# One expert's x in fp32 by SyncE instead of two by SyncE and ScalarE, and the other one in the GpSimd queue

## The chip, the core and the metric

The kernel runs on one core of a Trainium2 chip. The metric is the device time of one execution in microseconds (us); lower is better. A core has five engines that run side by side: TensorE (PE in the profile, with its weight loads as PEld), VectorE (DVE), ScalarE (ACT), GpSimd (POOL) and SyncE (SP). Data come and go by 16 DMA engines that all queues share. In this kernel three engines issue transfers: SyncE and ScalarE each into a queue whose descriptors hardware makes (q1 and q10 in the profile), GpSimd into a queue whose descriptors its own cores write (q0). Only the transfers that GpSimd issues convert fp32 to fp16 on the way.

## The reference

Eight experts, each with 256 rows of x, a hidden size of 512 and an inner size of 2048. All inputs and the output are fp32.

```python
n_experts, capacity, hidden, expert_hidden = 8, 256, 512, 2048
# x (8, 256, 512), w1 (8, 512, 2048), w2 (8, 2048, 512), b1 (8, 2048), b2 (8, 512)
h = np.matmul(x, w1) + b1[:, np.newaxis, :]
h = np.maximum(h, 0)
return (np.matmul(h, w2) + b2[:, np.newaxis, :]).astype(np.float32)
```

## The kernel before

**Data.** Each expert has 4 MB of w1 and 4 MB of w2 in fp32 and 512 KB of x. The kernel multiplies in fp16. `load_w1` (L73) and `load_w2` (L79) fetch a whole expert's weights in one transfer from GpSimd, which writes 2 MB of fp16; `load_x` (L67) does the same with x and writes 256 KB. Three buffers hold w1, three hold w2, four hold x in fp16 (`x16`).

**Two experts' x come another way.** For experts 0 and 1 (`nXF32 = 2`) x is fetched as it stands, in fp32, into the tile `x32` (L188): expert 0's by SyncE, expert 1's by ScalarE. VectorE then copies each into its `x16` tile (L201, a cast). ScalarE also issues the fetch of b1 (L189), as 16 rows of 1024 numbers.

**Work on an expert.** `transposes(e)` (L96) turns x on TensorE by eight products with a unit matrix, and VectorE copies the result to `xT` (L106). `first_product(e)` (L108) makes 16 blocks of h with four products each (L113); ScalarE adds b1 and clips at zero (L120). Midway, after block 8, it calls `transposes(e + 1)`. `second_product(e)` (L151) puts b2 into two sums (L163) and adds 32 products of h and w2 (L175); VectorE and ScalarE copy the sums out (L138, L139). The second product runs three experts behind the first (`LAG = 3`).

**Before the first product** b1 must be turned as well: 64 small products with a unit matrix (L206), which GpSimd makes (`make_identity`, shown as masks.py:197 and 199), and two copies (L214). These stand ahead of `transposes(0)` on TensorE.

**The order of the transfers** is written out by hand. GpSimd issues w1 of expert 0 and b2 (L191) first, then makes the two unit matrices, and then takes the list `ring` in order: w1 of expert 1, x of expert 2, w1 of expert 2, x of expert 3, w1 of expert 3, w2 of expert 0, and so on. Outputs of seven experts are written back from the same list (`flush`, L130), and w2 of expert 7 comes in eight pieces (L88). GpSimd holds an issue back until the buffer is free and until the transfer eight places earlier in its queue has landed, as the kernel's eight completion semaphores for this queue are used in turn. The output of expert 7 leaves from SyncE and ScalarE (L142, L143, L149).

Of the kernel before, what the change touches and what calls it, by code (L numbers as in the profile page):

```python
# [11 lines left out]
def kernel(  # L12
# [9 lines left out]
    nc = tc.nc  # L22
# [5 lines left out]
    nTB = T // P  # L28
# [4 lines left out]
    LATE = (5, 6)  # L33
    RING = (0, 1, 2, 3, 4) + LATE
    PARTS = {}
    nXF32 = 2

    def ordered(ins):
        return tc.keep_in_program_order(ins)
# [17 lines left out]
    b1_rows = singles.tile([E * 2, M // 2], fp32)  # L57
# [15 lines left out]
    def load_w1(e):  # L73
        w1_sb[e] = w1_pool.tile([P, nKC, M], fp16, tag="w1", name="w1sb")
        ordered(nc.gpsimd.dma_start(  # L75
            out=w1_sb[e], in_=w1[e].rearrange("(p kc) m -> p kc m", kc=nKC)
        ))
# [107 lines left out]

    x32 = singles.tile([P, nXF32, nTB, H], fp32)
    for e in range(nXF32):
        (nc.sync if e == 0 else nc.scalar).dma_start(out=x32[:, e], max_dma_last_dim=2048, in_=x[e].rearrange("(p tb) h -> p tb h", tb=nTB))  # L188
    nc.scalar.dma_start(out=b1_rows, in_=b1.rearrange("e (s i) -> (e s) i", s=2))  # L189
    load_w1(0)  # L190
    ordered(nc.gpsimd.dma_start(  # L191
        out=b2_sb,
        in_=b2.rearrange("e h -> (e h)").rearrange("(o f) -> o f", o=1),
# [10 lines left out]
    for j in range(nJ):  # L204
        for s in range(2):
            ordered(nc.tensor.matmul(  # L206
                out=pb[s * 64 : (s + 1) * 64, j, :, :],
# [5 lines left out]
    for s in range(2):  # L213
        nc.vector.tensor_copy(  # L214
            out=b1T[s * 64 : (s + 1) * 64, :, :], in_=pb[s * 64 : (s + 1) * 64, :, :, s]
# [15 lines left out]
    e = E - LAG - 1  # L231
# [50 lines left out]
```

## Time and profile before

| | |
|---|---|
| time, median of 4 runs | 183.41 us (183.28 to 183.55) |
| the profiled execution: its time, and its span from first to last instruction | 183.55 us, 181.8 us |
| PE, PEld busy | 139.5 us (77%), 99.2 us (55%) |
| ACT, POOL, DVE busy | 62.9 us, 22.1 us, 13.4 us |
| moved by DMA, counted where it is written | 40.58 MB in 7017 packets |
| read from and written to HBM | 71.39 MB, 4.19 MB |
| granted TensorE clock | 0.924 of full speed |

The times of instructions and transfers are from this one profiled execution, counted from the start of its span; 1.75 us of its time lie outside the span. A packet is what one DMA engine moves in one go. The share of a queue is the time that its packets took, divided by 16 engines and by the stretch of time; packets overlap a little at their ends, and a packet counts in the stretch where it starts, so that a short stretch can show more than 100%.

### The profile page before, as it was taken

How to read it: one execution, taken by the hardware profiler on the slowest of the kernel's cores; microseconds unless marked ns; L12 is line 12 of the kernel's file. 1: busy time of each engine (PE TensorE's matmuls, PEld its weight loads, DVE VectorE, ACT ScalarE, POOL GpSimd, SP SyncE). 2: the span in 40 equal slices, each digit the busy share in tenths (PEclk: the TensorE clock that was granted, in tenths of full speed). 3: DMA queues.
4: the chain of work that ended last, by engine and by line, in shares of the span. 5: the costliest groups of instructions: out<-in, count | busy, mean ns of one | idle time of the engine just before them, and what ended most of it. 6: DMA issues, size and time to landing. Idle time of an engine off the chain costs nothing.

```text
span 181.8 us, 2204 instructions
## 1 busy us (share of the span) xinstructions
PE 139.5 (77%) x946; PEld 99.2 (55%) x946; DVE 13.4 (7%) x22; ACT 62.9 (35%) x138; POOL 22.1 (12%) x46
## 2 busy tenths in 40 slices
PE   0555999489650999649991899909999994999990
PEld 0544889479540845637481754907559641334670
DVE  0320011001000101010100101001010010000110
ACT  0022689548560421706063240723309501010100
POOL 7100021300300011111010000200004003113300
PEclk9999999979995699979999579996999999699999
DMA  5999999999999989999999999999999999999995
GB/s 182 280 195 225 231 209 195 209 253 213 193 231 231 213 191 231 198 234 202 231 231 191 213 231 231 173 288 206 198 231 224 274 195 278 211 242 282 218 279 191
DMA packets 7017, 40.58 MB, mean 223 GB/s; under 512 B 1216, under 2 KB 2256, under 8 KB 4960
## 3 DMA queue, kind: packets, MB, share of 16 engines
q0 software_dynamic: 5872, 38.81, 97.8%
q1 hardware_dynamic: 688, 0.95, 1.7%
q10 hardware_dynamic: 448, 0.69, 1.0%
q8 instruction: 7, 0.11, 0.2%
q14 instruction: 2, 0.02, 0.0%
HBM read 71.39 MB, written 4.19 MB: 416 GB/s over the span
## 4 chain that ended last, share of the span: by engine, by line
DMA 58%; PE 24%; issue 9%; another core or an unknown queue 3%; POOL 2%; ACT 0%; POOLq 0%
DMA x<-in_x_dram 24%; DMA w2sb<-in_w_dram 21%; PE acc L175 17%; DMA w1sb<-in_w_dram 13%; PE ph L113 6%; PE acc L163 1%; PE psx L100 1%; POOL w2sb L85 1%; POOL w1sb L75 1%; POOL out_dram L132 0%; POOL b_sb L191 0%; POOL ident masks.py:199 0%; POOL ident masks.py:197 0%; ACT out L139 0%
## 5 line engine op out<-in xcount | busy, mean ns | idle before, releaser
L113 PE MATMUL ph<-xT,w1sb 128*128 128x256 f16 x512 | 69.3, 302 | 8.7 <-DMA w1sb<-in_w_dram 8.7
L120 ACT ACTIVATE hT<-ph,b1T 128x256 f16<-128x256 f32 x128 | 57.1, 474 | 43.6 <-PE ph L113 43.4
L113 PEld LDWEIGHTS <-w1sb 128*128 128x128 f16 x512 | 62.1, 149 | 15.1 <-DMA w1sb<-in_w_dram 9.6
L175 PE MATMUL acc<-w2sb,hT 128*128 128x512 f16 x224 | 51.2, 388 | 2.3 <-DMA w2sb<-in_w_dram 2.3
L175 PEld LDWEIGHTS <-hT 128*128 128x128 f16 x288 | 27.6, 99 | 32.8 <-issue 7.7
L139 ACT COPY out<-acc 128x512 f32<-128x512 f32 (+2 forms) x9 | 4.9, 541 | 60.1 <-PE acc L175 60.1
L100 PE MATMUL psx<-ident,x 128*128 128x128 f16 x64 | 6.6, 265 | 20.1 <-DMA x<-in_x_dram 19.5
L100 PEld LDWEIGHTS <-x 128*128 128x128 f16 x64 | 5.3, 128 | 21.2 <-DMA x<-in_x_dram 20.4
L75 POOL DMA_DIRECT2D w1sb<-in_w_dram x8 | 4.4, 554 | 60.3 <-PE ph L113 59.5
L106 DVE COPY xT<-psx 128x1024 f16<-128x1024 f16 x8 | 5.5, 692 | 81.8 <-PE psx L100 81.8
L138 DVE COPY out<-acc 128x512 f32<-128x512 f32 (+2 forms) x9 | 5.7, 632 | 73.5 <-PE acc L175 73.5
L85 POOL DMA_DIRECT2D w2sb<-in_w_dram x8 | 4.3, 536 | 48.8 <-PE acc L175 48.8
L206 PE MATMUL pb<-ident,b_rows 16*64 16x16 f32 x64 | 3.7, 265 | 6.7 <-DMA b_rows<-in_b_dram 6.7
L175 PE MATMUL acc<-w,hT 128*128 128x320 f16 (+1 forms) x64 | 7.3, 273 | 0.0
L206 PEld LDWEIGHTS pb<-ident,b_rows 16*64 16x64 f32 x64 | 3.6, 198 | 6.7 <-issue 6.7
L91 POOL DMA_DIRECT2D w<-in_w_dram x8 | 5.0, 621 | 12.5 <-DMA w2sb<-in_w_dram 9.6
L132 POOL DMA_DIRECT2D out_dram<-out x7 | 3.8, 541 | 22.0 <-ACT out L139 13.1
L120 ACT ACT_TABLE_LOAD x1 | 1.3, 1283 | 11.1 <-DVE b1T L214 11.1
L163 PE MATMUL acc<-b_sb,ones 1*128 1x512 f16 (+2 forms) x18 | 4.8, 355 | 0.0
L69 POOL DMA_DIRECT2D x<-in_x_dram x6 | 3.3, 545 | 6.1 <-DMA w2sb<-in_w_dram 5.6
L163 PEld LDWEIGHTS <-ones 1*128 1x128 f16 x18 | 1.1, 92 | 2.2 <-issue 2.1
L201 DVE CAST x<-x 128x1024 f16<-128x1024 f32 x2 | 1.4, 694 | 4.4 <-DMA x<-in_x_dram 4.3
(9 smaller groups left out, 2.6 us busy)
## 6 DMA issues: line engine op xcount, KB each, us to landing
w1sb<-in_w_dram POOLq DMA_DIRECT2D x8, 2048.0 KB, 33.7
w2sb<-in_w_dram POOLq DMA_DIRECT2D x6, 2048.0 KB, 46.1
out_dram<-out POOLq DMA_DIRECT2D x7, 512.0 KB, 28.3
w2sb<-in_w_dram POOLq DMA_DIRECT2D x2, 1024.0 KB, 25.3
x<-in_x_dram POOLq DMA_DIRECT2D x6, 256.0 KB, 39.0
w<-in_w_dram POOLq DMA_DIRECT2D x2, 384.0 KB, 19.2
x<-in_x_dram SPq DMA_DIRECT2D x1, 512.0 KB, 4.5
x<-in_x_dram ACTq DMA_DIRECT2D x1, 512.0 KB, 5.3
```

What stands on the lines that cost most here:

```text
L75: ordered(nc.gpsimd.dma_start(out=w1_sb[e], in_=w1[e].rearrange("(p kc) m -> p kc m", kc=nKC)))
L85: ordered(nc.gpsimd.dma_start(out=t[:, lo : lo + step, :], in_=src[:, lo : lo + step, :]))
L91: ordered(nc.gpsimd.dma_start(out=t, in_=src[:, lo:hi, c0:c1]))
L100: ordered(nc.tensor.transpose(out=pt[:, kc, tb * P : (tb + 1) * P], in_=x16[e][:, tb, :].rearrange("p (q kc) -> p q kc", kc=nKC)[:, :, kc] ...
L106: nc.vector.tensor_copy(out=xT[e], in_=pt)
L113: ordered(nc.tensor.matmul(out=ph, lhsT=w1_sb[e][:, kc, :].rearrange("p (q j) -> p q j", j=nJ)[:, :, j], rhs=xT[e][:, kc, :], start=(kc == 0),
L120: nc.scalar.activation(out=hT[e][:, j, :], in_=ph, func=mybir.ActivationFunctionType.Relu, bias=b1T[:, j, e : e + 1], scale=1.0,)
L138: nc.vector.tensor_copy(out=out_sb[:, 0, :], in_=po[0])
L139: nc.scalar.copy(out=out_sb[:, 1, :], in_=po[1])
L163: ordered(nc.tensor.matmul(out=t, lhsT=ones1, rhs=b2_sb[0:1, e * H + c0 : e * H + c1], start=True, stop=False,))
L175: ordered(nc.tensor.matmul(out=acc[c0, tb], lhsT=hT[e][:, j, tb * P : (tb + 1) * P], rhs=t[:, j - lo, c0 - p0 : c1 - p0], start=False, sto ...
L206: ordered(nc.tensor.matmul(out=pb[s * 64 : (s + 1) * 64, j, :, :], lhsT=b1_rows.rearrange("r (q j) -> r q j", j=nJ)[:, :, j], rhs=ident[0 ...
```

## The change

`nXF32` becomes 1. Expert 0's x is fetched by SyncE in fp32 as before, and the fetch of b1 goes to SyncE behind it. ScalarE issues no transfer at the start any more. Expert 1's x is fetched by `load_x(1)`, which becomes the first entry of `ring`: GpSimd issues it ahead of w1 of expert 1, and it is converted on the way. The `x32` tile is half as large, and one cast on VectorE is gone. In the changed kernel's list of instructions by engine, SyncE has one more, ScalarE two fewer, VectorE one fewer and GpSimd one more; TensorE has the same in the same order.

```diff
-    nXF32 = 2
+    nXF32 = 1
...
     x32 = singles.tile([P, nXF32, nTB, H], fp32)
     for e in range(nXF32):
-        (nc.sync if e == 0 else nc.scalar).dma_start(out=x32[:, e], max_dma_last_dim=2048, in_=x[e].rearrange("(p tb) h -> p tb h", tb=nTB))
-    nc.scalar.dma_start(out=b1_rows, in_=b1.rearrange("e (s i) -> (e s) i", s=2))
+        nc.sync.dma_start(
+            out=x32[:, e], max_dma_last_dim=2048, in_=x[e].rearrange("(p tb) h -> p tb h", tb=nTB)
+        )
+    nc.sync.dma_start(out=b1_rows, in_=b1.rearrange("e (s i) -> (e s) i", s=2))
     load_w1(0)
```

## The prediction

> **What bounds the kernel now.** I read the page's rows by slice and queue first, then the chain that ended last, then the timeline and the DMA queues of the first microseconds, because only those are touched.
>
> From the page: the busy share of the 16 DMA engines in 40 slices of 4.5 us, and the queues with packets, MB and share of the span.
>
> ```profile
> DMA  5999999999999989999999999999999999999995
> q0 software_dynamic: 5872, 38.81, 97.8%
> q1 hardware_dynamic: 688, 0.95, 1.7%
> q10 hardware_dynamic: 448, 0.69, 1.0%
> ```
>
> After the first slice the DMA engines never rest, and GpSimd's queue q0 fills them. Twenty-microsecond stretches from 40 to 160 us give a DMA share of 0.99 to 1.04. So the end moves with the sum of what the engines carry and with the time at which they begin, not with any one wait of TensorE. The chain of waits, in order of time (start, duration, what), agrees:
>
> ```profile
> 3.29 22.90 DMA w1sb<-in_w_dram
> ...
> 114.94 38.31 DMA w2sb<-in_w_dram
> 153.25 0.04 issue
> 153.29 8.75 PE acc L175 x32
> ```
>
> The long links are transfers waiting in the queue behind others. From 153.29 TensorE works almost without a pause until 177.4, but the start of that stretch is set by a landing of w2, and the last piece of w2 lands at 176.8, just ahead of its products. If q0 as a whole shifts, both shift.
>
> The timeline of the start (start, duration, engine, operation, in brackets the idle time before):
>
> ```profile
> 0.74 0.43 SPq L188 DMA_DIRECT2D x<-in_x_dram  x1
> 0.74 0.50 ACTq L188 DMA_DIRECT2D x<-in_x_dram  x1
> 1.26 0.67 POOL L75 DMA_DIRECT2D w1sb<-in_w_dram  x1 [0.81 <-POOLq L266]
> 1.27 0.49 ACTq L189 DMA_DIRECT2D b_rows<-in_b_dram  x1
> 15.58 6.85 PE L113 MATMUL ph<-xT,w1sb 128*128 128x256 f16 x36 [3.44 <-DMA w1sb<-in_w_dram]
> ```
>
> GpSimd has issued expert 0's w1 by 1.93. But the queues show when its packets move. First the stretch 1.5 to 2.9 us, then 3.0 to 4.5 (packets, MB, share):
>
> ```profile
> q1 hardware_dynamic: 80, 0.16, 63.2%
> q10 hardware_dynamic: 6, 0.01, 4.1%
> ```
>
> ```profile
> q1 hardware_dynamic: 149, 0.31, 52.1%
> q10 hardware_dynamic: 145, 0.30, 51.4%
> ```
>
> And the stretch 5.14 to 5.45, the first one in which q0 appears at all:
>
> ```profile
> q0 software_dynamic: 16, 0.26, 406.5%
> q10 hardware_dynamic: 35, 0.04, 35.1%
> ```
>
> From 3.0 on x of both experts fills all 16 engines, 294 packets in 1.5 us. The first 16 packets of q0, one for each engine, start in the 0.3 us in which q10 (x of expert 1, then b1) runs out. Before 2.9 the engines were not full and q0 moved nothing, so w1 became ready somewhere between 2.9 and 5.14; the trace does not say where. This is the open number.
>
> **The change part by part.**
>
> *Expert 1's x leaves the hardware queue.* It is 512 KB in packets of 2 KB, 256 of them. At 294 packets in 1.5 us, 196 a microsecond, they take 256 / 196 = 1.31 us of all engines. Without them x of expert 0 and b1 run out 1.31 us earlier: instead of about 5.3 (the middle of the stretch above) at about 4.0.
>
> *The slow beginning.* In 1.5 to 2.9 only 86 packets start, with a share of 67%; the stretch 2.5 to 3.0 has 62%, so 0.19 us there are idle, in which expert 0's x alone does not fill the engines. Descriptors for both x's are being made in that time. If those of expert 1 no longer compete, part of it may come back: 0 to 0.19, and I take 0.1. So the engines would be free for q0 at about 3.9.
>
> *Expert 1's x enters q0 between b2 and expert 1's w1.* The price has a row: expert 2's x does the same in this trace, behind expert 1's w1. Of the issues in the stretch 2.9 to 3.9 (KB each, us from issue to landing):
>
> ```profile
> w1sb<-in_w_dram POOLq DMA_DIRECT2D x1, 2048.0 KB, 22.9
> x<-in_x_dram POOLq DMA_DIRECT2D x1, 256.0 KB, 23.6
> ```
>
> The first was issued at 3.29 and landed at 26.2; the second, issued at 3.85, landed at 27.45. The x in the ring cost 1.25 us. Its packets give nearly the same: in 24.9 to 25.7 all of q0's packets but three are of this x, 80 in 0.8 us, and 128 of them (half of 256, as fp16 is half as long) take 1.28. I take 1.25.
>
> *When w1 is ready.* If by 3.9, q0 starts as soon as the engines are free, and no time is lost. If later, the engines rest until then. Bounds: ready at 2.9, cost 0; ready only at 5.15, cost 5.15 - 3.9 = 1.25. I take 0, by the nearest rows: SyncE's x was issued from 0.74 and its first packets come in the stretch 1.5 to 2.0, about 1 us later. ScalarE's, issued at the same time, appears only at the end of 1.5 to 2.9, some 2 us later. For q0, ready at 3.9 would be 2.6 us from the issue at 1.26, more than either; ready at 5.15 would be 3.9.
>
> On this the Trainium skill can be heard, in "DMA: Bandwidth & Descriptors". Its table of specifications gives the first byte of a GpSimd transfer as about 1 us and of a SyncE one as about 0.6; the first is an estimate of readiness near 2.9 from the end of issue at 1.93, and by it the gap is nothing. Its section on queues, rings and completion order says that a DMA engine takes turns between the queues that have work, packet by packet. That speaks against this change: a w1 that was ready at 3 would have had turns between the packets of x, and the trace shows none before 5.14. By that rule w1 was not ready earlier, the gap is 1.25, and the sum would be slower by 1.1. I do not follow it, because with q0 ready by chance on each engine just as that engine's last x or b1 packet ended, some engine should show a pause, and from 5.14 to 6.3 the shares of q0 (108.6%) and q10 (9.4%) leave no room for one.
>
> *Issues moved.* On SyncE b1 is issued behind x (0.43 us), at about 1.2 instead of 1.27; nothing else is on SyncE until 177. ScalarE loses two issues that ended at 1.76; its first work is at 11.1. GpSimd's issue of 0.55 us for x moves w1 of expert 1 from 3.29 to 3.84, and those behind it likewise; expert 0's w1 keeps the engines busy long after that, and GpSimd's next issue waits for TensorE at 26.24 anyway. All at nothing. The semaphores used in turn move by one place, and each later issue waits for the same partner as before; only expert 4's w1 now follows x of expert 1 instead of b2, both landed long before 34.2.
>
> *VectorE and TensorE.* One cast of 0.69 us goes, off the path: TensorE waited for b1 (6.6), not for it. b1 ends about 1.3 earlier, and the chain b1 (3.7 us), copies, `transposes(0)`, copy to `xT` ends near 11.5 instead of 12.9; w1 lands near 14.2 instead of 15.5. The cover of 2.7 us stays. Expert 1's x lands about 15.5 (w1, then 1.25), and is wanted at block 8 of the first product, 6.6 us after 14.2. Cover 5 us; nothing. If the chain to `xT` lost its cover, TensorE would start late, but would still wait for expert 1's w1 at 26.2, as now (0.3 us).
>
> **Sum.** -1.31 - 0.10 + 1.25 + 0 = -0.16 us. Expert 1's w1 lands where it does now, 26.2, or 0.1 to 0.2 earlier, and so does all behind it. The profiled execution would go from 183.55 to 183.4; it lies 0.14 above the median, so the median goes from 183.41 to 183.25. No change that a measurement of this kernel can tell: that needs 0.2%, 0.37 us.
>
> **Rivals.**
>
> *Slower: a hole ahead of w1.* Same trade, but q0 is not ready at 3.9. It costs what it is late: 0.5 us late gives -0.16 + 0.5, 183.75; at worst -0.16 + 1.25 = +1.1, 184.5. It decides against the kernel from a readiness of about 4.45 on (0.37 + 0.16 behind 3.9). For it: q0 shows nothing before 5.14, although three queues could share. Against: the first packets of q0 come on the heels of q10.
>
> *Faster: the slow beginning shrinks.* In 1.8 to 2.9 the engines started 86 packets where full speed would be 216, so 0.66 us of them is lost to the start. If the hardware serves one x much better than two, all of that could come back: -1.31 - 0.66 + 1.25 = -0.7, 182.7. For it: x of expert 0 moves at half speed until x of expert 1 sets in. Against: the first packets are slow before x of expert 1 is in flight. Over 0.37 it needs the engines free, and w1 ready, by 3.7.
>
> *Slower for another reason.* TensorE's clock falls below full speed in some slices; another such stretch after 153 would push the end by itself, as the last stretch has no slack. Or x of expert 1 lands too late, which would need 5 us. Some tenths each, up to 184.2.
>
> **Chances.** The forecast's case has 0.53: most of it (0.43) within 0.37 us, 0.10 faster, as the term of 0.1 may be larger. The slow beginning 0.12, faster. The hole 0.30 and the other reasons 0.05, slower. That makes 0.22 faster, 0.43 no change, 0.35 slower. The forecast's own range is 182.95 to 183.6. The range for 8 in 10 goes to 182.9, which leaves out the far end of the faster rival, and to 184.4, which leaves out the last of the hole.
>
> **What would show it.** Right: q0's first packets near 3.9 with no idle stretch before, w1 of expert 0 landing near 14.2, x of expert 1 about 1.25 later, the products of expert 1 starting at 26.1 to 26.2, span 181.6. The hole: DMA idle between about 4 and the first packet of q0, and expert 1's products later than 26.24 by as much as the hole. Faster: q0's packets before 3.7. Wrong in another way: w1 of expert 1 lands on time and yet the end moves.

## The result, and the profile after

The change made the kernel slower: 184.56 us (median of 34 runs, 183.54 to 185.63) against 183.49 us (54 runs, 183.18 to 184.15), a ratio of 1.0052 with a 95% interval of 1.0042 to 1.0062, about 1 us. The forecast was 183.25 and no change. The changed kernel's runs lie in a band of 2.1 us, those of before in one of 1.0, and its best runs come within 0.1 us of before's median: what was lost is not a fixed amount. The profiled execution took 184.49 us with a span of 182.7 us, 0.9 us longer than before.

From the page of the changed kernel, the DMA engines' busy tenths and the queues (packets, MB, share of the span):

```profile
DMA  7989999999999999999999998999999999999994
q0 software_dynamic: 6016, 39.07, 98.3%
q1 hardware_dynamic: 720, 1.02, 1.7%
q10 hardware_dynamic: 144, 0.10, 0.2%
```

The move was made as described: q10 has lost 0.59 MB, q0 has gained 0.26 MB and 144 packets, and the first slice is busier, 7 tenths instead of 5, because q0 starts earlier. The engines are nearly always busy, as before. Nothing here tells of a loss.

The timeline of the changed kernel (start, duration, engine, operation, idle time before), the start and the first products of experts 0 and 1:

```profile
1.24 0.45 SPq L191 DMA_DIRECT2D b_rows<-in_b_dram  x1
1.25 0.67 POOL L75 DMA_DIRECT2D w1sb<-in_w_dram  x1 [0.81 <-POOLq L268]
3.29 0.56 POOL L69 DMA_DIRECT2D x<-in_x_dram  x1
15.87 6.46 PE L113 MATMUL ph<-xT,w1sb 128*128 128x256 f16 x36 [5.24 <-DMA w1sb<-in_w_dram]
...
26.87 4.16 PE L113 MATMUL ph<-xT,w1sb 128*128 128x256 f16 x36 [1.03 <-DMA w1sb<-in_w_dram]
```

w1 of expert 0 was to land near 14.2, earlier by the 1.3 us that left the hardware queues. TensorE begins at 15.87, later than the 15.58 of before, and the products of expert 1, forecast for 26.1 to 26.2, begin at 26.87. The timeline of before has there:

```profile
26.24 4.16 PE L113 MATMUL ph<-xT,w1sb 128*128 128x256 f16 x36 [0.30 <-DMA w1sb<-in_w_dram]
```

Now the queues in four consecutive stretches of the changed kernel; first 3.4 to 4.0 us:

```profile
q0 software_dynamic: 14, 0.23, 188.9%
q1 hardware_dynamic: 74, 0.12, 53.3%
```

4.0 to 4.4 us (q0's line alone here and in the next two):

```profile
q0 software_dynamic: 2, 0.03, 62.6%
```

4.5 to 5.4 us:

```profile
q0 software_dynamic: 15, 0.25, 132.2%
```

6.6 to 7.3 us:

```profile
q0 software_dynamic: 1, 0.02, 11.0%
```

This is where the time went. 16 first packets, one for each DMA engine: 14 start between 3.56 and 4.0, on the heels of x and b1, even a little earlier than forecast. The last one starts at 4.36 and takes 2726 ns, where all the other first packets take 1226 to 1391 ns. So 15 engines are at their second packet by 5.4 us, and the sixteenth comes to its second one at 7.06, the lone packet of the last stretch. In before, all 16 first packets started within 0.3 us and took 1226 to 1346 ns.

The records of the single packets say more. The hardware queue has 32 packets of 4 bytes here, 16 for x and 16 for b1, which I read as the close of each engine's part of a transfer. Of the 16 that close b1, 15 are followed by a first packet of q0 within 0.02 us. The one left over is the earliest and ends at 3.54. The trace does not number the engines, but by this the sixteenth was the first to run out of work, stood idle for 0.8 us until 4.36, and then needed 1.5 us more than the shortest for its first packet. In before no engine pauses: each of the 16 first packets starts as one of b1's closing packets ends, to within 0.01 us.

What one late engine means is seen in the landings. The trace counts the completion of a transfer engine by engine; the table gives when the first, the fifteenth and the last engine were through (us):

| | before | after |
|---|---|---|
| w1 of expert 0 | 15.13 / 15.53 / 15.54 | 13.73 / 14.17 / 15.82 |
| w1 of expert 1 | 24.88 / 25.24 / 26.20 | 24.73 / 26.21 / 26.82 |
| last piece of w2 | 175.20 / 176.78 / 176.82 | 175.17 / 177.03 / 177.74 |

The first engine is where the sum put it, 0.15 us ahead of before at w1 of expert 1 and level at the end. Before has one engine 0.96 us behind the fifteenth there, at 26.20; after's fifteenth, 26.21, may be the same one. The last engine is 0.6 to 0.9 us behind, and a transfer has landed when its last engine is through: TensorE starts at 15.87, behind 15.82. The Trainium skill says the same, "DMA: Bandwidth & Descriptors", section on why a DMA increments its semaphore by 16: the engines finish independently and each posts its own count. The table agrees, with 2.09 us between the first and the last engine.

The chain of waits of the changed kernel and its last stretch in the timeline:

```profile
3.84 22.98 DMA w1sb<-in_w_dram
...
154.55 19.21 DMA w<-in_w_dram
173.76 0.04 issue
173.80 2.89 PE acc L175 x24
```

```profile
171.95 1.47 PE L175 MATMUL acc<-w,hT 128*128 128x320 f16 x12 [0.75 <-DMA w<-in_w_dram]
173.80 4.47 PE L175 MATMUL acc<-w,hT 128*128 128x320 f16 x36 [0.38 <-DMA w<-in_w_dram]
```

In before TensorE ran from 153.29 almost without a pause, and had all 64 products of these pieces in one stretch:

```profile
170.06 7.29 PE L175 MATMUL acc<-w,hT 128*128 128x320 f16 x64
```

Now the pieces come too late for it twice, 0.75 and 0.38 us, and the last products end 0.92 us later, as the last landing does.

That the end follows the last landing holds for every kernel below. In all 19 profiled executions, time less landing of the last piece's last engine is 6.69 to 6.82 us (before 183.55 - 176.82 = 6.73, after 184.49 - 177.74 = 6.75), while the times go from 183.20 to 187.10.

### The profile page after: what moved, and what is told of

The parts are those of the page before. It is cut to its first block, busy times and chain, and to the rows that moved or that the text cites. A ratio compares the mean times of both kernels' runs of the same rounds, so it can differ in the third digit from the quotient of the medians.

```text
span 182.7 us, 2203 instructions
## 1 busy us (share of the span) xinstructions
PE 138.1 (76%) x946; PEld 98.5 (54%) x946; DVE 12.7 (7%) x21; ACT 62.7 (34%) x138; POOL 22.8 (12%) x47
## 3 DMA queue, kind: packets, MB, share of 16 engines
HBM read 71.39 MB, written 4.19 MB: 414 GB/s over the span
## 4 chain that ended last, share of the span: by engine, by line
DMA 71%; PE 22%; POOL 2%; issue 1%; ACT 1%; ACTq 0%; POOLq 0%
DMA x<-in_x_dram 24%; DMA w2sb<-in_w_dram 24%; DMA w1sb<-in_w_dram 13%; PE ph L113 11%; DMA w<-in_w_dram 11%; PE acc L175 10%; PE psx L100 1%; PE acc L163 1%; POOL w1sb L75 1%; ACT out L139 1%; POOL ident masks.py:199 0%; POOL out_dram L132 0%; POOL b_sb L193 0%; POOL w L91 0%; POOL x L69 0%
## 5 line engine op out<-in xcount | busy, mean ns | idle before, releaser
L175 PE MATMUL acc<-w2sb,hT 128*128 128x512 f16 x224 | 49.5, 379 | 1.1 <-DMA w2sb<-in_w_dram 1.1
L175 PEld LDWEIGHTS <-hT 128*128 128x128 f16 x288 | 27.1, 98 | 32.0 <-issue 6.1
L175 PE MATMUL acc<-w,hT 128*128 128x320 f16 (+1 forms) x64 | 7.8, 272 | 1.2 <-DMA w<-in_w_dram 1.1
L69 POOL DMA_DIRECT2D x<-in_x_dram x7 | 3.8, 547 | 5.9 <-DMA w2sb<-in_w_dram 4.5
L203 DVE CAST x<-x 128x1024 f16<-128x1024 f32 x1 | 0.7, 742 | 3.7 <-DMA x<-in_x_dram 3.7
```

The lines of the kernel that those rows point to most:

```text
L175: ordered(nc.tensor.matmul(out=acc[c0, tb], lhsT=hT[e][:, j, tb * P : (tb + 1) * P], rhs=t[:, j - lo, c0 - p0 : c1 - p0], start=False, sto ...
```

## The experiments

Theories for the late engine, with the letters that the expectations use:

- **A**: GpSimd issues x and w1 from 3.29 to 6.08, just when q0 now starts, and that disturbs it.
- **B**: q0 starts too soon after its own issue, and is not ready on every engine.
- **C**: b1 behind x on SyncE, on one hardware queue.
- **D**: no late engine matters; x in the ring costs more than 1.25 us.
- **E**: the hand-over from a hardware queue that runs out to q0.
- **F**: the time since the program began.
- **G**: what stands ahead of q0: one hardware queue that runs dry soon, instead of two.

Ratios are to before, measured beside it on the same chip, with 95% intervals.

**1. Later issues in the changed kernel (`after_hold`).** GpSimd waits for b1's copy before it goes on with the ring, so its issues come from 9.32 us on.

```diff
 transposes(0)
+hold = singles.tile([1, 1], fp32)
+ordered(nc.gpsimd.tensor_copy(out=hold, in_=b1T[0:1, 0, 0:1]))
```

> The changed kernel, but GpSimd copies one number of b1T (ready at 9.5 us in the changed kernel's trace) before it issues x of expert 1 and what follows, so that it issues nothing between 2.4 and 9.5 us, while q0 starts. Theory A (GpSimd's issues at 3.29 to 6.08 us, made while q0 starts at 3.55 to 4.36, hold up one of the 16 DMA engines, whose first q0 packet took 2726 ns against 1226 to 1391 on the others): no such packet, w1 of expert 0 lands near 14.3 us instead of 15.8, expert 1's products start near 26.1, and the time is some 0.2 us under before, 183.3, with runs within 0.3 us of each other. Theory B (q0's first packets are slow on one engine because they no longer stand ready behind another transfer, whoever issues then): the slow first packet stays, w1 lands at 15.5 to 16 and the time stays near 184.5 with the same spread.

Measured: 184.84 us (6 runs, 184.04 to 185.53), 1.0066 (1.0042 to 1.0090). First packets of up to 2036 ns with no issue near them. The profiled execution is the fastest of the six, and its last engine landed w1 of expert 0 at 14.71, which neither theory had named; by the times of all six A falls.

**2. Issues at q0's start in the kernel before (`before_late_issue`).** The reverse: they are put on 5.85 us and later, where before's first packets run.

```diff
+hold = singles.tile([1, 1], fp32)
+ordered(nc.gpsimd.tensor_copy(out=hold, in_=x32[0:1, 0, 0, 0:1]))
```

> The kernel before, but GpSimd copies one number of x32 of expert 0 (landed at 5.26 us in the trace of before) before it issues w1 of expert 1 and the three transfers behind it. They then fall into about 5.4 to 7.6 us, while q0 starts (5.15 to 5.42), instead of 3.29 to 5.44. Theory A: one engine's first or second q0 packet becomes slow here too, w1 of expert 0 lands up to 1.5 us after 15.5, and the time grows by 0.5 to 1.2 us with a wider spread, to about 184.3. Theory B: w1's packets still stand ready behind x of expert 1, and nothing changes: 183.5.

Measured: 183.55 us (11 runs), 0.9999 (0.9990 to 1.0007). A falls again.

**3. The old cover with the new ring (`after_cover`).** ScalarE fetches expert 1's x in fp32 as before, into a tile that nobody reads, and b1 behind it; x of expert 1 also stays in the ring.

```diff
+spare = singles.tile([P, nTB, H], fp32)
-nc.sync.dma_start(out=b1_rows, ...)
+nc.scalar.dma_start(out=spare, max_dma_last_dim=2048, in_=x[1].rearrange(...))
+nc.scalar.dma_start(out=b1_rows, ...)
```

> The changed kernel, but ScalarE also fetches x of expert 1 in fp32 as before, into a tile that nothing reads, and b1 behind it. q0 then starts near 5.3 us as in before, and only the 1.25 us of expert 1's x in q0 are added. Both theories: first packets of q0 all near 1226 ns; w1 of expert 0 at 15.5, expert 1's products 1.25 us later than in before, at 27.5; time before + 1.25 = 184.7, narrow spread. If the x in q0 cost much less or more than 1.25, the price of the ring was misjudged; if the spread stays as wide as in the changed kernel, the late start of q0 is not what makes it even.

Measured: 184.68 us (5 runs, 184.50 to 184.96), 1.0063 (1.0050 to 1.0076), 1.20 us above before. The start is even again (first packets of 1226 to 1259 ns, w1 of expert 0 landing from 15.18 to 15.60), and the last engine is through with expert 1's w1 at 27.49, 1.29 after before's 26.20. Its timeline, expert 1:

```profile
27.54 2.73 PE L113 MATMUL ph<-xT,w1sb 128*128 128x256 f16 x23 [2.57 <-DMA w1sb<-in_w_dram]
```

So x in the ring costs 1.2 to 1.3 us with an even start, as taken from the row. D falls.

**4. b1 back on ScalarE (`after_b1_scalar`).**

```diff
-nc.sync.dma_start(out=b1_rows, in_=b1.rearrange("e (s i) -> (e s) i", s=2))
+nc.scalar.dma_start(out=b1_rows, in_=b1.rearrange("e (s i) -> (e s) i", s=2))
```

> The changed kernel with b1 issued by ScalarE as before, and only x of expert 0 by SyncE. A third theory, C: the slow engine is one that carries a late packet of b1 behind x in the same queue. C: the slow first packet goes and the time is 183.3. A and B: nothing changes, near 184.5 with runs from 183.5 to 185.6.

Measured: 183.22 us (11 runs, 183.07 to 183.52), 0.9984 (0.9976 to 0.9993). It is the fastest of the three, by 0.26 us against before. Its stretch 4.0 to 4.4 us:

```profile
q0 software_dynamic: 16, 0.26, 306.5%
q1 hardware_dynamic: 49, 0.07, 48.1%
```

and its timeline, the first products of experts 0 and 1:

```profile
14.37 5.93 PE L113 MATMUL ph<-xT,w1sb 128*128 128x256 f16 x36 [4.92 <-DMA w1sb<-in_w_dram]
...
26.49 4.16 PE L113 MATMUL ph<-xT,w1sb 128*128 128x256 f16 x36 [2.67 <-DMA w1sb<-in_w_dram]
```

All 16 first packets within 4.06 to 4.33 us, each 1226 ns, and w1 of expert 0 lands from 14.03 to 14.33. This is the start that the forecast had described, 0.3 to 0.5 us later than the changed kernel's own, and the time that it had named. C was now the favourite.

**5. b1 behind x on SyncE in the kernel before (`before_b1_sync`).**

```diff
-nc.scalar.dma_start(out=b1_rows, ...)
+nc.sync.dma_start(out=b1_rows, ...)
```

> The kernel before with one part of the change alone: b1 is issued by SyncE behind x of expert 0; x of expert 1 stays with ScalarE in fp32. Theory C (b1 behind x in SyncE's queue makes one engine late, wherever the rest stands): slow first q0 packets, w1 of expert 0 landing 0.4 to 1.5 us after 15.5, time 183.9 to 184.6 with a spread of over 1 us. Theory B (q0's first packets are slow when the hardware queues run out before about 4 us, as q0 is then only just ready, and b1's place matters only through that time): q0 starts at about 5.2, first packets of 1226 ns, no change, 183.5.

Measured: 183.49 us (11 runs), 1.0006 (0.9997 to 1.0014). b1's place alone does no harm.

**6. No b1 on a hardware queue (`after_b1_gpsimd`).** GpSimd fetches b1 behind w1, SyncE has x of expert 0 alone.

```diff
-nc.sync.dma_start(out=b1_rows, ...)
 load_w1(0)
+ordered(nc.gpsimd.dma_start(out=b1_rows, ...))
```

> The changed kernel, but b1 is fetched by GpSimd behind w1 of expert 0 (unconverted), so that SyncE fetches x of expert 0 alone and no hardware queue carries b1. The hardware queue runs out at about 3.5, q0 starts there. Theory C: clean first packets of 1226 ns, w1 of expert 0 lands at 13.9, evenly. Theory B: slow first packets as in the changed kernel or worse, landings of w1 apart by over 0.6 us, the last engine at 14.5 to 15.8. As b1 lands behind w1 and its turning takes some 6 us, TensorE's first product starts at about 20 instead of 15; w1 of expert 1 is there at 26.2 and the first product then ends at about 30, 4 us late, which the later stages should take up. Time: C 183.1, B 183.5 to 185.

Measured: 184.37 us (7 runs, 183.45 to 185.45), 1.0055 (1.0028 to 1.0082). In the stretches 3.5 to 3.9 and 5.1 to 5.3 us:

```profile
q0 software_dynamic: 15, 0.25, 305.2%
```

```profile
q0 software_dynamic: 1, 0.02, 80.0%
```

The sixteenth engine starts at 5.21 us and needs 2561 ns, with no b1 on any hardware queue. Read as above, it had closed its part of x at 3.51, the first of the 16, and stood idle for 1.7 us. The profiled execution is the slowest of the seven. C falls.

**7. The good version, w1 issued later (`scalar_b2_first`).** b2 is issued ahead of w1, whose issue moves from 1.25 to 1.91 us.

```diff
 # after_b1_scalar, and:
-load_w1(0)
 ordered(nc.gpsimd.dma_start(out=b2_sb, ...))
+load_w1(0)
```

> The changed kernel with b1 on ScalarE (183.22 us, q0's first packets at 4.06 to 4.33, all of 1226 ns), but GpSimd issues b2 before w1 of expert 0, which is so issued 0.5 us later, at about 1.8. Theory B: w1 is ready 0.5 us later than before, at about the time when the hardware queues run out (4.1 to 4.3), so slow first packets of 1300 to 2700 ns come back, w1 of expert 0 lands at 15 to 16 instead of 14.3, and the time is 183.7 to 184.6 with a wider spread. Theory C: nothing changes, 183.2.

Measured: 185.06 us (6 runs, 184.61 to 185.65), 1.0094 (1.0076 to 1.0112). Stretches 4.3 to 4.5 and 5.3 to 5.45 us (41 packets, since b2's small ones stand ahead of w1's):

```profile
q0 software_dynamic: 41, 0.25, 614.5%
```

```profile
q0 software_dynamic: 1, 0.02, 91.5%
```

With b1 on ScalarE the late engine is back: it starts w1 at 5.38, the others by 4.44. That spoke for B, a lead that is too short.

**8. The same without b2 ahead (`scalar_w1_late`).** The unit matrices are made first, and w1 is issued at 1.72 us.

```diff
 # after_b1_scalar, and:
+make_identity(nc, ident)
+make_identity(nc, ident16)
+late = singles.tile([1, 1], fp32)
+ordered(nc.gpsimd.tensor_copy(out=late, in_=ident[0:1, 0:1]))
 load_w1(0)
```

> The changed kernel with b1 on ScalarE, but GpSimd makes the unit matrices first and then issues w1 of expert 0, at about 2.4 to 2.8 instead of 1.26. This measures how long after its issue w1 is ready, as the engines are idle by then. Theory B: first packets 2.2 to 2.6 us after the issue, at 4.8 to 5.3, behind a hole of 0.5 to 1.0 us, and slow; time 184 to 184.8. Theory C: ready about 1.7 us after the issue, at 4.1 to 4.5, a hole of 0.3 at most, clean packets, 183.2 to 183.6.

Measured: 183.75 us (10 runs), 1.0033 (1.0006 to 1.0059), but the runs fall apart: five at 183.20 to 183.34, five at 184.17 to 185.29. The profiled one is of the first kind, with first packets at 4.19 to 4.43 us. So w1 can be ready on all engines within 2.7 us of its issue, and yet half the runs lose a microsecond.

**9 and 10. A filler behind b1 on SyncE (`after_fill_128k`, `after_fill_256k`).** 128 or 256 KB of x in fp32, read by nobody, were to keep the hardware queue going for longer.

```diff
+spare = singles.tile([P, H], fp32)
+nc.sync.dma_start(out=spare[0:64], max_dma_last_dim=2048, in_=x[1]...[0:64, 0, :])   # or [0:128]
```

> The changed kernel (b1 on SyncE behind x) with one more transfer on SyncE behind b1: 128 KB of x in fp32 into a tile that nothing reads, 64 packets of 2 KB, 0.33 us of all engines. Theory B, as it stands now: w1 of expert 0 is ready on 15 engines by 2.3 us after GpSimd issues it (at 1.26), on the last one only some 2.7 to 3.1 us after (4.0 to 4.4), and a q0 that starts earlier pays on that engine with a first packet of 1.9 to 2.7 us. With the filler the hardware queue runs out at about 3.9 to 4.2: between the two, median 183.4 to 184.4, smaller spread than in the changed kernel. Theory D (the changed kernel's loss comes from x in q0 alone, dearer than 1.25 us): the time grows by 0.33 over the changed kernel, 184.8.

> As the kernel with 128 KB more, with 256 KB: 128 packets, 0.65 us. The hardware queue runs out at about 4.3 to 4.5. Theory B: all first packets of q0 near 1226 ns, the last landing of w1 of expert 0 within 0.4 us of the first, at about 14.6, narrow spread; the engines carry 0.65 us more than in the changed kernel, and yet the time falls from 184.5 to about 183.4 to 183.8. Theory D: 0.65 more than the changed kernel, 185.2.

Measured: 184.62 us (6 runs), 1.0062 (1.0041 to 1.0083), and 184.64 us (9 runs), 1.0060 (1.0034 to 1.0086). Neither tests what it was made for: q0 started at 3.6 us all the same, before the filler. The stretch 5 to 8 us of the first:

```profile
q0 software_dynamic: 41, 0.67, 106.0%
q1 hardware_dynamic: 27, 0.06, 5.4%
```

The filler's packets go singly between q0's packets. Inconclusive for B and G, but they show the queues taking turns.

**11 and 12. The kernel before, w1 issued later (`before_w1_late`, `before_w1_later`).** The unit matrices and a memset come first; w1 is issued at 2.71 and at 3.15 us, with the hardware queues as in before.

```diff
 # before, and ahead of load_w1(0):
+make_identity(nc, ident)
+make_identity(nc, ident16)
+late = singles.tile([P, 2 * H], fp32)        # 3 * H in the second
+nc.gpsimd.memset(late, 0.0)
+ordered(nc.gpsimd.tensor_copy(out=late[0:1, 0:1], in_=ident16[0:1, 0:1]))
```

> The kernel before, with x of both experts in fp32 by the hardware queues and b1 on ScalarE, but GpSimd makes the unit matrices and fills a spare tile before it issues w1 of expert 0, so at about 2.8 us instead of 1.26. The hardware queues still run out at 5.15 to 5.42, now 2.4 to 2.6 us behind that issue, as in the changed kernel (2.3 to 2.6). Theory B: the late engine appears here too, though nothing of the change is in it: one engine's first q0 packet starts late or takes 1.9 to 2.7 us, the last landing of w1 of expert 0 is 1 to 2 us behind the first, time 184.0 to 185 with a spread of over 1 us. If it depends on when q0 starts after the start of the program and not after its issue, nothing changes: 183.5.

> As the kernel before with w1 issued late (2.71 us there), but with more to fill on GpSimd, so that w1 of expert 0 is issued at about 3.2 and q0 starts some 2.0 us behind the issue. Theory B: most runs now have the late engine or a hole ahead of q0; median 184 to 185, spread over 1 us. Theory E, or a rule by the time since the start of the program: 183.6 as with the issue at 2.71.

Measured: 183.58 us (12 runs), 1.0007 (0.9994 to 1.0020), with three of the runs above 183.9; and 183.58 us (12 runs), 1.0005 (0.9990 to 1.0020). In the second q0 starts at 5.18 us, 2.0 us after its issue; in the changed kernel the lead was 2.3, in `scalar_b2_first` 2.4. A shorter lead does no harm here: B falls, as far as it is a rule of the lead. That one engine was not ready when its hardware queue ran out stays, for the changed kernel.

**13. q0 with nothing ahead of it (`start_queue_alone`).** w1, x of expert 0, b1 and b2 are all issued by GpSimd.

```diff
-    nXF32 = 1
+    nXF32 = 0
 ...
-nc.sync.dma_start(out=b1_rows, ...)      # and x of expert 0
 load_w1(0)
+load_x(0)
+ordered(nc.gpsimd.dma_start(out=b1_rows, ...))
```

> The changed kernel with no transfer on SyncE and ScalarE at the start: GpSimd issues w1 of expert 0 at 1.26 us and behind it x of expert 0, b1 and b2. No other queue is there to hide or delay q0, so the first packet of each engine shows when that engine has its share of w1. Theory B (readiness after the issue differs by engine): most engines start between 2.9 and 3.5 us, one or two at 4.0 to 5.4 or with a first packet of 1.9 to 2.7 us. Theory E (all are ready together, and it is the hand-over from the hardware queue that disturbs an engine): 16 first packets within 0.3 us of each other, 1226 to 1400 ns. The time itself tells little: x of expert 0 and b1 come late and TensorE starts late, 184 to 188.

Measured: 184.45 us (6 runs, 184.20 to 184.59), 1.0045 (1.0029 to 1.0061). The stretches 2.6 to 3.0 and 3.0 to 4.3 us:

```profile
q0 software_dynamic: 15, 0.25, 464.8%
```

```profile
q0 software_dynamic: 1, 0.02, 8.2%
```

w1, issued at 1.26, has its first packets at 2.65 to 2.96 us, 1.4 us after the issue, and one engine follows at 3.59. All 16 first packets take 1715 to 2235 ns, and every second one after them 1226 to 1250. There is no hand-over from another queue here, so slow first packets and a late engine do not need one: E falls as the whole cause.

**14 and 15. A filler on ScalarE from the start (`after_fill_act_128k`, `after_fill_act_256k`).** The same fillers, issued by ScalarE beside x of expert 0; b1 stays on SyncE.

```diff
+spare = singles.tile([P, H], fp32)
+nc.scalar.dma_start(out=spare[0:64], max_dma_last_dim=2048, in_=x[1]...[0:64, 0, :])   # or [0:128]
```

> The changed kernel (b1 on SyncE behind x) and 128 KB of x in fp32, 64 packets, issued by ScalarE at 0.74 into a tile that nothing reads, so that it moves beside x of expert 0 and ahead of q0's start, 0.33 us of all engines. q0 starts at about 3.9 to 4.2, 2.6 to 2.9 us behind w1's issue. Theory B: fewer runs with the late engine than in the changed kernel; median 183.5 to 184.2. Theory E: 184.5 and 0.33 more, 184.8.

> As the kernel with 128 KB by ScalarE, with 256 KB, 128 packets, 0.65 us. q0 starts at about 4.2 to 4.5, 2.9 to 3.2 us behind w1's issue. Theory B: no late engine, narrow spread, and although the engines carry 0.65 us more than in the changed kernel the time falls from 184.5 to 183.5 to 183.9. Theory E: 184.5 and 0.65 more, 185.2.

Measured: 184.11 us (12 runs, 183.44 to 184.81), 1.0031 (1.0013 to 1.0050), and 184.08 us (12 runs, ten of them 183.94 to 184.22), 1.0035 (1.0024 to 1.0047). The small filler leaves the start uneven; w1 of expert 0 lands from 14.17 to 16.00. With the larger one q0 starts at 4.64 us or later, w1 lands from 14.69 to 15.37, and the band is nearly gone. It moves 256 KB more than the changed kernel, for nothing, and still does not come out slower: 1.0035 against the changed kernel's 1.0052, with intervals that overlap a little.

**16. Everything 1 us later (`after_all_later`).** A memset ahead of the fetches of x, b1 and w1.

```diff
+nc.gpsimd.memset(x32, 0.0)
+late = singles.tile([P, H], fp32)
+nc.gpsimd.memset(late, 0.0)
+ordered(nc.gpsimd.tensor_copy(out=late[0:1, 0:1], in_=late[0:1, 1:2]))
 ...                                       # x, b1 and w1 follow in this order
```

> The changed kernel, but GpSimd first fills the tile x32 (SyncE's fetch of x of expert 0 waits for that, b1 stands behind it) and a spare tile, so that x and b1 move some 1.0 us later and w1 of expert 0 is issued some 1.0 us later too. q0 starts at about 4.6 to 4.9 us instead of 3.55 to 3.9, with the same things ahead of it. Theory F (time since the program's start decides): no late engine; the whole start costs 1.0, so 183.5 + 1.0 = 184.5, narrow spread. Theory G (what stands ahead of q0, one queue that runs dry): the late engine stays, 185.5, spread over 1 us.

Measured: 186.16 us (6 runs, 184.59 to 187.10), 1.0140 (1.0109 to 1.0171). q0 starts at 4.53 us, as late as in good kernels, and is uneven: w1 of expert 0 lands from 15.46 to 18.40. Five first packets come late, and here the engine that closed b1 first is not among them: it starts q0 at once, at 4.53. F falls.

**17. Two hardware queues, little data (`after_x0_split`).** Expert 0's x in halves by SyncE and ScalarE, b1 on SyncE.

```diff
+nc.sync.dma_start(out=x32[:, e, 0], ...[:, 0, :])
+nc.scalar.dma_start(out=x32[:, e, 1], ...[:, 1, :])
```

> The changed kernel, but x of expert 0 is fetched in two halves, by SyncE and by ScalarE, at the same time; b1 stays on SyncE behind its half. The same bytes move ahead of q0, on two hardware queues. q0 starts at 3.4 to 4.0. Theory F: as uneven as the changed kernel, 184.0 to 185. Theory G in the form that two queues keep q0 from stumbling: even, first packets near 1226 ns, 183.2 to 183.5.

Measured: 184.37 us (6 runs, 183.77 to 184.72), 1.0044 (1.0027 to 1.0061). First packets of up to 2525 ns. That two queues are ahead of q0 is not what helps: this form of G falls.

**What is left.** One quantity sorts nearly all of them: how long the hardware queues have been moving data (their first packet comes at 1.8 us, in `after_all_later` at 2.8) when q0's first packet starts.

| hardware queues running for | kernels | start |
|---|---|---|
| 2.8 us or more | before, `before_b1_sync`, `before_late_issue`, `after_cover`, `after_fill_act_256k`, `before_w1_later` | even, or nearly |
| the same | `before_w1_late` | even in 9 of 12 runs by their times |
| 2.25 to 2.5 us | `after_b1_scalar`; `scalar_w1_late`; `scalar_b2_first` | even; half; uneven |
| 1.7 to 2.0 us | after, `after_hold`, `after_b1_gpsimd`, both fillers on SyncE, `after_fill_act_128k`, `after_all_later`, `after_x0_split` | uneven |
| 0 | `start_queue_alone` | all first packets slow, one engine late |

It is a pattern, read after the runs, and not a cause. In the middle row the kernel that starts earliest is the best one and the latest the worst. In the changed kernel and in `after_b1_gpsimd` the late engine is the one that ran out first, in `after_all_later` it is others, so that is no rule either. What makes an engine wait, and what then makes its first packet long (descriptors not yet there, the memory, or something in the engine), no trace here shows, nor which engine it is. That stays open.

## Why the prediction was wrong

**Step by step.** *Expert 1's x leaves the hardware queue, -1.31, and the slow beginning, -0.10*: right, the second rather too small. q0's first packets were named for 3.9 and started at 3.56 to 4.05 on 15 engines; the fifteenth engine landed w1 of expert 0 at 14.17, where 14.2 was named. *x in the ring, +1.25*: right, 1.20 in time and 1.29 in landing by `after_cover`. *Issues moved, VectorE, TensorE, at nothing*: right; `after_hold` and `before_late_issue` moved the issues with no gain and no loss, and the first product's wait is for w1 still. *The clock*: 0.93 after, 0.924 before; no part of it.

**The step that failed** is "When w1 is ready", taken at 0. It had one readiness for the whole queue, and asked whether that lay before or after 3.9. The runs show 16 starts that differ. For 15 engines the answer 0 was right; the sixteenth stood idle from 3.54 to 4.36, had a first packet of twice the length, and was 1.8 to 2.2 us behind the others at its second (7.06 against 4.90 to 5.31). Since each transfer waits for its slowest engine, 0.6 us of that were seen against before at expert 1's w1 and 0.92 at the last landing, which is the 0.94 between the two profiled executions. In the terms of the sum: -0.16 stands (`after_b1_scalar`, with an even start, came 0.26 us below before), and in place of the 0 there belongs about 1.1, the slowest engine's loss.

**The rivals.** "A hole ahead of w1" named the right place and, with its 184.5 at worst, the right size, but not what happened: it looked for one hole on all DMA engines ahead of q0's first packet, and 3.4 to 4.0 us shows q0 on 14 engines at once, with the hole on one. The prediction had asked for just that sign, a pause on some engine, and looked for it in before, where there is none. The price was bounded by the start of before, 1.25, as if nothing could be worse than starting as late as before; one engine was worse. Hence a range that ended at 184.4, below the median.

**Turns between queues.** The prediction set aside the rule of the Trainium skill, "DMA: Bandwidth & Descriptors" (queues, rings and completion order), that an engine takes turns between queues with work, since by it a w1 not seen before 5.14 was not ready. About the readiness it was right to, for 15 engines: the same issue at 1.25 had packets at 3.56 in the changed kernel and at 2.65 in `start_queue_alone`. The turns themselves were seen with the filler, and not while x was in flight: in the changed kernel too, q0 started on each of those 15 engines only as its hardware queue ran out. What the prediction had from before, that all engines started together, was a property of a start behind 3.3 us of other traffic, and it was carried over to one behind 1.7.

## What to carry to other kernels

In a kernel bound by its DMA engines a queue is as late as its slowest engine: read the first and the last engine of a landing, not only the queue's share, and give each engine its own line in the sum. Moving x between the queues was near to neutral by its bytes (1.31 us against 1.25), so what decided was how the long queue started. One line, b1 back to ScalarE, turned a change that cost 0.5% into one that gains 0.16% (0.07 to 0.24) over the kernel before.

## What the runs showed of the hardware

- Most of what one engine loses at 4 us is still lost at 177 us. The changed kernel and `after_b1_scalar` differ in who issues b1, and in their profiled executions the last engine is 1.49 us apart at w1 of expert 0 (15.82 and 14.33) and 1.23 at the last landing (177.74 and 176.51). Not always so much: `after_x0_split` is 2.51 behind at the first (16.84) and 1.21 at the last (177.72).
- First packets of 16 KB took 1715 to 2235 ns on all engines where nothing ran ahead of the queue, and 1226 to 1346 ns in before, behind 3.3 us of other traffic.
- In before q0 had no packet until 5.14 us, while two x's were in flight, though w1 issued at the same time had its first at 2.65 us in `start_queue_alone` and at 3.56 in the changed kernel; yet later, single filler packets did get in between q0's.
- Expert 0's x is faster alone: in the stretch 1.5 to 2.9 us SyncE's queue starts 133 packets in the changed kernel, where both x's together had started 86 in before.

The slow beginning did shrink, which the faster rival had supposed; the slowest engine took the gain and more.
